# Up projection of a gated MLP in 1024-column groups with one seven-product pair each, its sums on VectorE, and the product of activation and gate on GpSimd

## The chip, the core and the metric

The kernel runs on one core of one Trainium2 chip. A core has five engines with an instruction queue each: TensorE (PE) multiplies 128x128 weights with up to 512 columns into a PSUM bank, VectorE (DVE) and ScalarE (ACT) work element by element on SBUF and PSUM, GpSimd (POOL) on SBUF, and SyncE (SP) here issues most of the DMA transfers. An engine works its queue strictly in order, and an instruction that waits for another engine holds up everything behind it. The metric is the device time of one launch in microseconds.

## What is computed

One layer of a decoder trunk on 256 tokens with a model width of 2048: a mixer of two groups of heads, a gated MLP and a per-layer embedding gate, each added to x. The change is in the MLP, which is, cut from the reference:

```
h = rms_norm(x) @ w_up            # 2048 -> 2 * 5632 columns: a | g
a = causal depthwise convolution of width 3 over the tokens, with bias
u = gelu(a) * g
x = x + u @ w_down                # 5632 -> 2048
```

All is float32.

## The kernel before

**Products.** TensorE takes operands of a rounded type, so each float32 operand is split in two, hi and lo, and a product is three matmuls: hi by hi, hi by lo, lo by hi. The weights stream through SyncE's queue from HBM into a ring of buffers named raw (128 rows of the contraction x 1024 numbers). ScalarE casts a raw to hi (L208), VectorE subtracts to get lo (L210). A block then is 12 matmuls of 512 columns: two halves of the tokens (T1 and T2, 128 each), two halves of the 1024 numbers, three matmuls each. Hi and lo are prepared some blocks ahead of TensorE, `run_stream` decides how many; that distance is called the lead here.

**Up projection.** There are 11 groups q. A group takes 512 columns of a and the same 512 of g, one after the other, with `token_group`: a raw holds two contraction blocks of 128 for 512 columns. So a group is 16 blocks, 8 for a and 8 for g, 192 matmuls; the operand of the tokens is x2T. As either half of a group ends, ScalarE brings its two PSUM banks out with the norm's scale into z (L918), and VectorE transposes them within 32x32 squares into the tile sq (L919).

**The job of a group.** `ffn_job(q)` runs beside the next group's products; two of its pieces are woven in after every block. It sends sq in 16 small transfers Y<-sq on SyncE (L931), so that columns stand on the partitions; ScalarE starts the convolution (L951), VectorE adds the two other taps in eight operations (L954); GpSimd makes the two first positions of each 32 (halo and E, L942 to L948), VectorE adds them (L960); ScalarE applies GELU in place (L962); VectorE multiplies by g in four operations (L966) into u; the split of u into hi (ScalarE, L129) and lo (VectorE, L130) goes into the tile uT. For six pairs of contraction blocks, of the groups 1 to 3 and 6 to 8, sums E3, E5, E6 and E7 of u are made on VectorE (L980) and split into the tile uE (L983, L984).

**Down projection.** After six up groups the first 20 contraction blocks of the down projection are multiplied, after all eleven the other 24, each for 1024 columns twice, with `quad_group`. Here a raw holds one contraction block for 1024 columns. A pair of contraction blocks is either two blocks of 12 (kind R), or a seven-product pair: of the eight products of a 2x2 by 2x2 block multiplication one is saved by sums on both sides (the Winograd form). Such a pair comes in four steps: o1 (two products), o2 (one), c1 (two) and c2 (two). Between o2 and c1 four sums of the raw weights are made in place on VectorE (L357), and c1 and c2 are cast anew from them. The products go to four banks qgD, of the 2x2 halves, and four banks qgQ, which are combined at the end (`down_mid`, L1056 to L1062). `weave` puts the pairs between the R blocks: a head of R blocks, and how many stand between the steps.

**What orders the work.** The instructions of every engine stand in the order in which the code's calls and a scheduler put them; names such as raw_6167 in the rows below number the buffers in order of the code. The rows 380 to 410 and their like are positions in an engine's queue.

Of the kernel before, what the change touches and what calls it, by code (L numbers as in the profile page):

```python
# [15 lines left out]
P = 128  # L16
# [21 lines left out]
QF = 24  # L38
SEVEN = ((3, 5, 7), (13, 15, 17))
PAD = 112  # L40


@with_exitstack
def layer_kernel(
# [18 lines left out]
    def f32(ap):  # L63
        return ap.bitcast(F32)
# [838 lines left out]
    with tc.tile_pool(name="ffn", bufs=1) as fp:  # L903
        uT = fp.tile([P, QF, 512], F32R, name="uT")
        uE = fp.tile([P, max(map(len, SEVEN)), 4, 256], F32R, name="uE")
        in_seven = {p: i for ps_ in SEVEN for i, p in enumerate(ps_)}
        rstd2 = rstd_of(ssq2, "ffn")
        halo = [fp.tile([P, 4, NT, 4, 2], F32, name=f"halo{i}") for i in range(2)]
        for h in halo:
            pool.memset(h, 0.0)  # L910
        sq = {}

        def up_evac(q, ag):
            def f(t, b):
# [3 lines left out]
                act.activation(z, b, AF.Copy, scale=rstd2[:, t : t + 1])  # L918
                dve.transpose(sq[q][:, ag, :, t].rearrange("p j f r -> p f j r"),  # L919
                              z.rearrange("p (f j c) -> p f j c", f=4, j=4))  # L920
                if ag == 1 and t == NT - 1:
                    side.append(ffn_job(q))
            return f

        def ffn_job(q):
# [39 lines left out]
            for f in range(4):  # L965
                dve.tensor_mul(u[:, f], c[:, :, :, f].rearrange("p i t r -> p t i r"),  # L966
                               g[:, :, :, f].rearrange("p i t r -> p t i r"))
            yield
# [3 lines left out]
            for p in (2 * q, 2 * q + 1):  # L972
                if p in in_seven:
# [32 lines left out]
        blocks = []  # L1006
        x2 = aT["cur"]

        def up(q):
            for ag in range(2):  # L1010
                blocks.extend(token_group(w_up, all_k, lambda: x2, ag * FF + q * 512, 512, up_evac(q, ag),
                                          tag=("mm", "aux")[ag]))

        def u_unit(p, name):
            if name[0] == "E":
                v = uE[:, in_seven[p], "3567".index(name[1])]
                return v[:, 0:128], v[:, 128:256]
# [13 lines left out]

        def tmp(i):
            return fp.tile([P, 512], F32, tag="z", name=f"t{i}", bufs=3)

        pT = {}

        def load_p():
            pr = tmp(3).rearrange("p (t d) -> p t d", t=NT)
            nc.sync.dma_start(out=pr, in_=p[0, 0].rearrange("(t p) d -> p t d", p=P))
            yield 6  # L1040
# [4 lines left out]
            pT["t"] = fp.tile([P, 2, 512], F32R, tag="c", name="pT")  # L1045
            for k in range(2):
                split_T(pT["t"][:, k, :], bk[:, k * 256 : (k + 1) * 256])
            yield

        def down_mid(c, ends):  # L1050
            def f(st):
                if ends and c == 0:
                    side.append(load_p())
                xc = [[xs[:, t, (c + n) * 512 : (c + n + 1) * 512] for n in range(2)] for t in range(NT)]
# [24 lines left out]
        def down(pairs, seven, ends, order):  # L1079
            for c in (0, 2):  # L1080
# [3 lines left out]
                cols = w_down[0][:, c * 512 : (c + 2) * 512].rearrange("k (h n) -> k h n", h=2)  # L1084
                tags = ("aux", "mm") if (c == 0) == ends else ("mm", "aux")
                grp = quad_group(lambda k, cols=cols: cols[k * P : (k + 1) * P], seq, u_unit, tags, down_mid(c, ends),
                                 down_end(c, ends))
                if c == 0:
                    st = grp[first]
                    st.fn = lambda hi, lo, fn=st.fn: (pull(10 ** 6), fn(hi, lo))  # L1090
                blocks.extend(grp)
# [13 lines left out]
        def gate_done(c0, n):  # L1105
            sg = {}

            def f(t, b, i=0, j=n):
                if "r" not in r3:
                    r3["r"] = rstd_of(ssq3, "ple")  # L1110
                if i == 0:
                    sg[t] = fp.tile([P, 512], F32, tag="z", name="sg", bufs=3)
                w = (j - i) // (2 if i else 1)
# [46 lines left out]
```

## Time and profile before

| | us |
|---|---|
| median of 3 runs | 1254.61 (1253.37 to 1256.06) |
| the profiled execution | 1254.04 |
| its span, first to last instruction | 1252.2 |
| TensorE busy | 1246.1, 5699 matmuls |
| VectorE busy | 808.4 |
| ScalarE busy | 662.6 |
| GpSimd busy | 35.8 |
| first up group to first down group | 434.2 to 697.2 |
| first down stage | 697.2 to 802.6 |
| up groups 6 to 10 | 802.6 to 1020.2 |
| second down stage | from 1020.2 |

The span is cut by what TensorE multiplies. A busy time is the sum of an engine's instructions; durations of matmuls overlap, so their cost is the distance of their starts. "Idle before" gives what an engine waited for ahead of a group of instructions, and an engine that is waited for by nobody may idle at no cost.

### The profile page before, as it was taken

The numbers are of one execution on the slowest core, as the hardware profiler recorded it, in microseconds if no ns is written. First come the engines' busy times: TensorE is split into PE (matmuls) and PEld (weight loads), VectorE is DVE, ScalarE is ACT, GpSimd is POOL, SyncE is SP. The second block draws the span as 40 slices with busy tenths as digits, with TensorE's granted clock in tenths as the row PEclk, the third lists the DMA queues.
The fourth block names the chain that finished last, engine by engine and source line by source line (L and its number), as shares of the span: only waits on it lengthen the run. The fifth ranks groups of instructions, "written<-read, shape, count | busy, mean of one in ns | idle before, by whom it ended". The sixth has DMA issues, their size and how long they took to land.

```text
span 1252.2 us, 16051 instructions
## 1 busy us (share of the span) xinstructions
PE 1246.1 (100%) x5699; PEld 1048.7 (84%) x5699; DVE 808.4 (65%) x1044; ACT 662.6 (53%) x918; POOL 35.8 (3%) x90
## 2 busy tenths in 40 slices
PE   9999999999999999999999999999999999999998
PEld 7899988888888888888888888888888888888887
DVE  6455566555565555676576697847577659978554
ACT  7555545445554555555465554445455546556542
POOL 2000000000000000000000000000000000000000
PEclk9999999999999999999999999999999999999999
DMA  8667877864567767677777675767767765787661
GB/s 286 173 180 219 255 237 216 209 180 137 162 185 196 236 222 218 202 224 218 212 223 226 186 241 169 234 190 215 231 200 230 222 193 185 222 217 247 205 210 51
DMA packets 161856, 258.77 MB, mean 207 GB/s; under 512 B 38377, under 2 KB 65905, under 8 KB 161777
## 3 DMA queue, kind: packets, MB, share of 16 engines
q1 hardware_dynamic: 161168, 257.57, 68.9%
q8 instruction: 44, 0.72, 0.2%
q14 instruction: 35, 0.29, 0.1%
q10 hardware_dynamic: 385, 0.16, 0.0%
q0 software_dynamic: 224, 0.03, 0.0%
HBM read 237.76 MB, written 2.12 MB: 192 GB/s over the span
## 4 chain that ended last, share of the span: by engine, by line
PE 99%; DMA 0%; SPq 0%; DVE 0%; ACT 0%; issue 0%; DVEq 0%
PE tg L288 26%; PE tg L289 26%; PE tg L290 26%; PE qgD L324 5%; PE qgD L325 5%; PE qgD L326 5%; PE qgQ L325 1%; PE qgQ L324 1%; PE qgQ L326 1%; PE xT L141 1%; PE mob L752 0%; DMA xs<-in_x_dram 0%; PE sc L633 0%; PE ob L661 0%; PE msc L727 0%; PE pt L654 0%
## 5 line engine op out<-in xcount | busy, mean ns | idle before, releaser
L210 DVE TENSOR_TENSOR lo<-raw,hi 128x1024 fp32r<-128x1024 f32 (+3 forms) x475 | 561.4, 1190 | 370.8 <-ACT hi L208 356.4
L208 ACT CAST hi<-raw 128x1024 fp32r<-128x1024 f32 (+3 forms) x475 | 482.6, 1025 | 455.1 <-PE tg L290 304.7
L288 PE MATMUL tg<-hi,x2T 128*128 128x512 f32 x704 | 274.1, 389 | 0.0
L290 PE MATMUL tg<-hi,x2T 128*128 128x512 f32 x704 | 274.0, 389 | 0.0
L289 PE MATMUL tg<-lo,x2T 128*128 128x512 f32 x704 | 273.9, 389 | 0.0
L288 PE MATMUL tg<-hi,hT 128*128 128x512 f32 (+2 forms) x480 | 181.8, 383 | 0.0
L289 PE MATMUL tg<-lo,hT 128*128 128x512 f32 (+2 forms) x480 | 180.3, 378 | 0.0
L290 PE MATMUL tg<-hi,hT 128*128 128x512 f32 (+2 forms) x480 | 180.2, 379 | 0.0
L289 PEld LDWEIGHTS tg<-lo,x2T 128*128 128x128 f32 x704 | 132.1, 188 | 27.5
L290 PEld LDWEIGHTS tg<-hi,x2T 128*128 128x128 f32 x704 | 132.1, 188 | 27.4
L288 PEld LDWEIGHTS tg<-hi,x2T 128*128 128x128 f32 x704 | 132.1, 188 | 27.3
L325 PE MATMUL qgD<-lo,uT 128*128 128x512 f32 x286 | 111.3, 389 | 0.0
L326 PE MATMUL qgD<-hi,uT 128*128 128x512 f32 x286 | 111.2, 389 | 0.0
L324 PE MATMUL qgD<-hi,uT 128*128 128x512 f32 x286 | 103.6, 389 | 0.0
L290 PEld LDWEIGHTS tg<-hi,hT 128*128 128x128 f32 x480 | 89.9, 188 | 12.7
L289 PEld LDWEIGHTS tg<-lo,hT 128*128 128x128 f32 x480 | 90.2, 188 | 12.2
L288 PEld LDWEIGHTS tg<-hi,hT 128*128 128x128 f32 x480 | 90.0, 188 | 12.0
L326 PEld LDWEIGHTS qgD<-hi,uT 128*128 128x128 f32 x286 | 53.7, 188 | 11.2
L324 PEld LDWEIGHTS qgD<-hi,uT 128*128 128x128 f32 x286 | 53.7, 188 | 11.2
L325 PEld LDWEIGHTS qgD<-lo,uT 128*128 128x128 f32 x286 | 53.7, 188 | 11.0
L289 PE MATMUL tg<-lo,x3T 128*128 128x512 f32 (+1 forms) x144 | 52.7, 366 | 0.0
L288 PE MATMUL tg<-hi,x3T 128*128 128x512 f32 (+1 forms) x144 | 52.7, 367 | 0.0
(227 smaller groups left out, 1093.3 us busy)
## 6 DMA issues: line engine op xcount, KB each, us to landing
raw<-in_w_up_dram SPq DMA_DIRECT2D x176, 512.0 KB, 4.6
raw<-in_w_down_dram SPq DMA_DIRECT2D x88, 512.0 KB, 4.7
raw<-in_w_in_dram SPq DMA_DIRECT2D x79, 512.0 KB, 4.3
raw<-in_w_out_dram SPq DMA_DIRECT2D x32, 512.0 KB, 4.3
raw<-in_w_ple_gate_dram SPq DMA_DIRECT2D x32, 512.0 KB, 4.7
Y<-sq SPq DMA_DIRECT2D x176, 64.0 KB, 3.2
raw<-in_w_in_dram SPq DMA_DIRECT2D x24, 416.0 KB, 3.6
raw<-in_w_in_dram SPq DMA_DIRECT2D x16, 408.0 KB, 3.7
```

Source lines behind the costliest of these rows:

```text
L141: pe.transpose(bk[:, t * P : (t + 1) * P], xs[:, t, k * P : (k + 1) * P], ident)
L208: act.copy(hi[:, :w], raw[:, :w])
L210: dve.tensor_sub(lo[:, :w], raw[:, :w], f32(hi[:, :w]))
L288: pe.matmul(bk[:, : e - c], ah, h[:, i, c:e], start=first, stop=False)
L289: pe.matmul(bk[:, : e - c], ah, l[:, i, c:e], start=False, stop=False)
L290: pe.matmul(bk[:, : e - c], al, h[:, i, c:e], start=False, stop=last)
L324: pe.matmul(st[bk], ah, hi[:, cols], start=first, stop=False)
L325: pe.matmul(st[bk], ah, lo[:, cols], start=False, stop=False)
L326: pe.matmul(st[bk], al, hi[:, cols], start=False, stop=final)
```

## The change

The groups q = 1 to 10 of the up projection are made with `quad_group` too: a raw is now one contraction block with 512 columns of a and 512 of g, and the four banks qgD are token half by a or g. Of the eight pairs of contraction blocks, pair 0 is a seven-product pair (`S_UP`), which stands behind four R blocks; its last two steps come after five more R blocks (`UP_ORDER`), and five follow. Its sums of x2 are made once, during group 0 (`x2_sums`, tile x2E). In place of ScalarE's evacuation, `up_mid` combines the four banks qgQ into three tiles and keeps them with the first, all scaled by the norm (ScalarE two operations out of PSUM and three in place, VectorE four out of PSUM), and `up_end` adds each bank qgD, scaled, to one of these (VectorE, four per group), and transposes it. All four banks of a group come to their end in its last block. Group 0 stays as it was.

The product of gelu(a) and g moves from VectorE to GpSimd. The result of the convolution now lies in the g half of the tile sq, which the transfers have emptied, instead of a tile of its own; the temporaries are four of one size; one of the four sums, E3, lies in a place of uT that is not needed (for one pair in uE); p is loaded earlier; the last group of the down projection has a head of five R blocks for four. The line numbers of the changed kernel: hi L211, lo L213, sums of raw L360, `up_mid` L952 to L959, `up_end` L968 and L969, transfers L993, convolution L1013 and L1016, edge L1022, GELU L1024, product L1028, split of u L132 and L133, sums of u L1042 to L1051.

```diff
+ONCE = (7,)
+S_UP = (0,)
+UP_ORDER = (4, (5,))
...
-        uE = fp.tile([P, max(map(len, SEVEN)), 4, 256], F32R, name="uE")
+        uE = fp.tile([P, 10, 256], F32R, name="uE")
...
+        def x2_sums():
+            for i, p in enumerate(S_UP):
+                a = tmp(0).rearrange("p (k s) -> p k s", k=2)
+                e = tmp(1).rearrange("p (e s) -> p e s", e=4)
+                x = x2[:, 2 * p : 2 * p + 2, :]
+                dve.tensor_add(a, f32(x[:, :, 0:256]), f32(x[:, :, 256:512]))
+                a11, a12, a21, a22 = a[:, 0, 0:128], a[:, 1, 0:128], a[:, 0, 128:256], a[:, 1, 128:256]
+                for dst, p0, p1 in ((e[:, 1], a21, a22), (e[:, 3], a21, a11), (e[:, 2], a11, e[:, 1]),
+                                    (e[:, 0], a12, e[:, 2])):
+                    dve.tensor_sub(dst, p0, p1)
+                yield
+                h = x2E[:, i].rearrange("p u (e s) -> p u e s", e=2)
+                act.copy(h[:, :, 0], e)
+                dve.tensor_sub(h[:, :, 1], e, f32(h[:, :, 0]))
+                yield
...
+        def up_mid(q):
+            def f(st):
+                t11, t12, t21, t22 = (tmp(i) for i in range(4))
+                act.copy(t22, st["Q1"])
+                act.activation(t11, st["Q1"], AF.Copy, scale=rstd2[:, 0:1])
+                dve.tensor_sub(t21, st["Q6"], t22)
+                dve.tensor_add(t12, st["Q5"], t21)
+                dve.tensor_add(t21, st["Q7"], t21)
+                dve.tensor_add(t22, st["Q7"], t12)
+                for v, r in ((t12, rstd2[:, 0:1]), (t21, nr[:, 1:2]), (t22, rstd2[:, 1:2])):
+                    act.activation(v, v, AF.Copy, scale=r)
+                comb[q] = (t11, t12), (t21, t22)
+            return f
+
+        def up_end(q):
+            def f(t, ag, b):
+                if t == 0 and ag == 0:
+                    sq[q] = fp.tile([P, 2, 4, NT, 4, 32], F32, tag="sq", name="sq")
+                z = comb[q][t][ag]
+                dve.scalar_tensor_tensor(out=z, in0=b, scalar=rstd2[:, t : t + 1], in1=z, op0=ALU.mult, op1=ALU.add)
+                dve.transpose(sq[q][:, ag, :, t].rearrange("p j f r -> p f j r"),
+                              z.rearrange("p (f j c) -> p f j c", f=4, j=4))
+                if ag == 1 and t == NT - 1:
+                    side.append(ffn_job(q))
+            return f
...
             for f in range(4):
-                dve.tensor_mul(u[:, f], c[:, :, :, f].rearrange("p i t r -> p t i r"),
-                               g[:, :, :, f].rearrange("p i t r -> p t i r"))
+                pool.tensor_tensor(out=u[:, f], in0=c[:, :, :, f].rearrange("p i t r -> p t i r"),
+                                   in1=g[:, :, :, f].rearrange("p i t r -> p t i r"), op=ALU.mult)
...
         def up(q):
-            for ag in range(2):
-                blocks.extend(token_group(w_up, all_k, lambda: x2, ag * FF + q * 512, 512, up_evac(q, ag),
-                                          tag=("mm", "aux")[ag]))
+            if q == 0:
+                for ag in range(2):
+                    blocks.extend(token_group(w_up, all_k, lambda: x2, ag * FF, 512, up_evac(q, ag),
+                                              tag=("aux", "mm")[ag]))
+                return
+            cols = w_up[0].rearrange("k (h n) -> k h n", h=2)[:, :, q * 512 : (q + 1) * 512]
+            seq = weave([p for p in range(KD // 2) if p not in S_UP], S_UP, *UP_ORDER)
+            blocks.extend(quad_group(lambda k: cols[k * P : (k + 1) * P], seq, x2_unit, tags(), up_mid(q), up_end(q)))
...
+        side.append(x2_sums())
         for q in range(6):
             up(q)
         down(range(0, 10), SEVEN[0], False, ((6, (3, 3)), (3, (3, 3, 3))))
         for q in range(6, KF // 4):
             up(q)
-        down(range(10, 22), SEVEN[1], True, ((6, (3, 2, 2)), (4, (3, 3, 3))))
+        down(range(10, 22), SEVEN[1], True, ((6, (3, 2, 2)), (5, (3, 3, 3))))
```

SyncE's queue at a group's end. Before (w_down is the next stage's weight), the transfers of the sixth group:

```order
L239 DMA raw_5989<-in_w_down_dram 128x1024
L931 DMA Y<-sq 32x2x256 x4
L239 DMA raw_6018<-in_w_down_dram 128x1024
L931 DMA Y<-sq 32x2x256 x4
L239 DMA raw_6044<-in_w_down_dram 128x1024
L931 DMA Y<-sq 32x2x256 x8
L239 DMA raw_6158<-in_w_down_dram 128x1024
```

Now, between two up groups:

```order
L242 DMA raw_7652<-in_w_up_dram 128x2x512
L242 DMA raw_7670<-in_w_up_dram 128x2x512
L993 DMA Y<-sq 32x2x256 x16
L242 DMA raw_7849<-in_w_up_dram 128x2x512
L242 DMA raw_7851<-in_w_up_dram 128x2x512
```

The sixteen transfers of an up group now stand in one run, with no weight among them.

VectorE's queue at an up group's end, in the change (t are the combined tiles, qgD the banks):

```order
L968 SCALAR_TENSOR_TENSOR t_5252<-qgD_5012,rstd_ffn,t_5252 128x512
L213 TENSOR_TENSOR lo<-raw_5243,hi 128x1024
L968 SCALAR_TENSOR_TENSOR t_5254<-qgD_5016,rstd_ffn,t_5254 128x512
L969 STREAM_TRANSPOSE sq<-t_5252 128x4x4x32
L968 SCALAR_TENSOR_TENSOR t_5253<-qgD_5020,rstd_ffn,t_5253 128x512
L968 SCALAR_TENSOR_TENSOR t_5255<-qgD_5024,rstd_ffn,t_5255 128x512
L969 STREAM_TRANSPOSE sq<-t_5254 128x4x4x32
L213 TENSOR_TENSOR lo<-raw_5287,hi 128x1024
L969 STREAM_TRANSPOSE sq<-t_5253 128x4x4x32
L969 STREAM_TRANSPOSE sq<-t_5255 128x4x4x32
```

Before, two transposes stood at the end of either half of the group; now four stand at the end of the whole, each behind a scale-and-add.

VectorE's queue in the first down stage, around the second seven-product pair, before:

```order
L966 TENSOR_TENSOR Y<-c,Y 128x256 x4
L210 TENSOR_TENSOR lo<-raw_6176,hi 128x1024
L210 TENSOR_TENSOR lo<-raw_6044,hi 128x512
L130 TENSOR_TENSOR uT<-Y,uT 128x4x256
L357 TENSOR_TENSOR raw_6044<-raw_6044 128x512
L210 TENSOR_TENSOR lo<-raw_6178,hi 128x1024
L357 TENSOR_TENSOR raw_6044<-raw_6044,raw_6158 128x512
L357 TENSOR_TENSOR raw_6158<-raw_6158,raw_6044 128x512
L357 TENSOR_TENSOR raw_6158<-raw_6158 128x512
L210 TENSOR_TENSOR lo<-raw_6044,hi 128x1024
L210 TENSOR_TENSOR lo<-raw_6158,hi 128x1024
```

And now:

```order
L360 TENSOR_TENSOR raw_6167<-raw_6167 128x512
L360 TENSOR_TENSOR raw_6167<-raw_6167,raw_6280 128x512
L133 TENSOR_TENSOR uT<-Y,uT 128x4x256
L360 TENSOR_TENSOR raw_6280<-raw_6280,raw_6167 128x512
L213 TENSOR_TENSOR lo<-raw_6167,hi 128x1024
L360 TENSOR_TENSOR raw_6280<-raw_6280 128x512
L213 TENSOR_TENSOR lo<-raw_6302,hi 128x1024
L213 TENSOR_TENSOR lo<-raw_6322,hi 128x1024
L1131 TENSOR_TENSOR xs<-qgQ_6324,xs 128x512
L213 TENSOR_TENSOR lo<-raw_6280,hi 128x1024
```

The split of u (L130, now L133) stood ahead of the pair's four sums and stands between the second and the third now; c1's lo and c2's (raw_6044 and raw_6158, now raw_6167 and raw_6280) stood together and are apart now, with two lo's and a residual sum between.

More of the change, by code (lines that the diff above doesn't have):

```diff
@@ new lines, in x2_unit @@
+        def x2_unit(p, name):
+            if name[0] == "E":
+                v = x2E[:, S_UP.index(p), "3567".index(name[1])]
+                return v[:, 0:128], v[:, 128:256]
+            t, k = int(name[0]) - 1, 2 * p + int(name[1]) - 1
+            return x2[:, k, t * P : (t + 1) * P], x2[:, k, 256 + t * P : 256 + (t + 1) * P]
+        nr = sm.tile([P, NT], F32, name="nr")
+        dve.tensor_scalar_mul(nr, rstd2, -1.0)
+        comb = {}
+        def up_mid(q):
[11 more added lines that the diff above has]
+            return f
@@ L981, in ffn_job @@
                     yield
-                    w = uE[:, in_seven[p]].rearrange("p u (e s) -> p u e s", e=2)
-                    act.copy(w[:, :, 0], e)
-                    dve.tensor_sub(w[:, :, 1], e, f32(w[:, :, 0]))
+                    n = 3 * in_seven[p]
+                    w = uE[:, n : n + 3].rearrange("p u (e s) -> p u e s", e=2)
+                    v3 = uE[:, 9] if p in ONCE else uT[:, 2 * p % QF]
+                    v3 = v3.rearrange("p (e s) -> p e s", e=2)[:, :, -128:]
+                    act.copy(w[:, :, 0], e[:, 1:4])
+                    act.copy(v3[:, 0], e[:, 0])
+                    dve.tensor_sub(w[:, :, 1], e[:, 1:4], f32(w[:, :, 0]))
+                    dve.tensor_sub(v3[:, 1], e[:, 0], f32(v3[:, 0]))
                     yield
@@ L1039, in load_p @@
             nc.sync.dma_start(out=pr, in_=p[0, 0].rearrange("(t p) d -> p t d", p=P))
-            yield 6
+            while "bank" not in pT:
+                yield 1
             bk = bank("mm", "pTp")
@@ L1052, in f @@
                 if ends and c == 0:
-                    side.append(load_p())
+                    pT["bank"] = True
                 xc = [[xs[:, t, (c + n) * 512 : (c + n + 1) * 512] for n in range(2)] for t in range(NT)]
@@ L1084, in down @@
                 cols = w_down[0][:, c * 512 : (c + 2) * 512].rearrange("k (h n) -> k h n", h=2)
-                tags = ("aux", "mm") if (c == 0) == ends else ("mm", "aux")
-                grp = quad_group(lambda k, cols=cols: cols[k * P : (k + 1) * P], seq, u_unit, tags, down_mid(c, ends),
+                grp = quad_group(lambda k, cols=cols: cols[k * P : (k + 1) * P], seq, u_unit, tags(), down_mid(c, ends),
                                  down_end(c, ends))
@@ L1090, in down @@
                     st.fn = lambda hi, lo, fn=st.fn: (pull(10 ** 6), fn(hi, lo))
+                    if ends:
+                        grp[0].fn = lambda hi, lo, fn=grp[0].fn: (fn(hi, lo), side.append(load_p()))
                 blocks.extend(grp)
+        side.append(x2_sums())
         for q in range(6):
@@ L1111, in f @@
                 if i == 0:
[L1112 removed]
+                    sg[t] = tmp(c0 // 256 + t)
                 w = (j - i) // (2 if i else 1)
```

23 lines of the change are left out of this document (14 added, 9 removed).

## The prediction

> **What bounds the kernel now.** I read the page first: the busy line of the engines and the chain that ended last.
>
> ```profile
> PE 1246.1 (100%) x5699; PEld 1048.7 (84%) x5699; DVE 808.4 (65%) x1044; ACT 662.6 (53%) x918; POOL 35.8 (3%) x90
> PE 99%; DMA 0%; SPq 0%; DVE 0%; ACT 0%; issue 0%; DVEq 0%
> ```
>
> TensorE works in all but 6.1 of the 1252.2 us of the span, and 99% of the chain lies on it. What a matmul costs is read from the timeline, since the mean duration of 389 ns overlaps with its neighbours:
>
> ```profile
> 808.74 0.39 PE L288 MATMUL tg<-hi,x2T 128*128 128x512 f32 x1
> ...
> 810.33 0.39 PE L289 MATMUL tg<-lo,x2T 128*128 128x512 f32 x1
> ```
>
> Seven starts in 1.59 us: one matmul of 512 columns costs 0.2271 us. An up group of 192 takes 192 x 0.2267 = 43.5 us (I use 0.2267, which the distance between the two rows 697.22 and 802.62 of the first down stage, 465 matmuls, gives: 105.4/465). So a matmul that goes away is worth 0.2267 us as long as its successors' operands are ready. Who makes them ready is in the table of stretches and the waits (columns: stretch, PE, PEld, DVE, ACT and POOL busy us with counts, clock, DMA):
>
> ```profile
> 437.00:480.00 43.00, 43.00 (x199) 35.61 (x198) 24.65 (x28) 21.81 (x28) 0.70 (x1) 1.00 0.69 222
> 480.00:523.00 43.00, 43.00 (x192) 35.59 (x191) 27.13 (x35) 24.36 (x27) 1.47 (x5) 1.00 0.73 219
> 523.00:567.00 44.00, 44.00 (x196) 36.44 (x195) 29.29 (x40) 23.55 (x28) 1.37 (x5) 1.00 0.72 215
> 697.00:751.00 54.00, 54.00 (x240) 44.72 (x239) 45.81 (x60) 29.55 (x33) 2.14 (x5) 1.00 0.69 216
> 1020.00:1080.00 60.00, 60.00 (x268) 49.69 (x267) 51.49 (x67) 33.61 (x39) 2.08 (x5) 1.00 0.69 212
> DVE lo L210 <- ACT hi L208: 356.4, 287, 4.6
> ACT hi L208 <- PE tg L290: 304.7, 208, 2.4
> ```
>
> In an up group VectorE works 27 to 29 us of 43.5; in the down stages, which already have seven-product pairs, 45.81 of 54 and 51.49 of 60 (85% and 86%), and TensorE still doesn't stand. The waits run backwards: VectorE waits for ScalarE's hi, and ScalarE for TensorE to free a buffer. The makers are ahead. Clock 1.00 and a DMA share of 0.7 are no bound.
>
> **The change part by part.** *Matmuls.* An up group of 16 blocks of 12 becomes 14 blocks of 12 and a pair of 6 + 3 + 6 + 6 = 21: 189 for 192. Ten groups: 30 matmuls less. 30 x 0.2267 = **-6.8 us**. Nothing else on TensorE changes its number.
>
> *VectorE and ScalarE, per up group.* The rows that price it:
>
> ```profile
> L210 DVE TENSOR_TENSOR lo<-raw,hi 128x1024 fp32r<-128x1024 f32 (+3 forms) x475 | 561.4, 1190 | 370.8 <-ACT hi L208 356.4 <-DMA Y<-sq 7.5 <-DMA raw<-in_w_in_dram 5.2
> L208 ACT CAST hi<-raw 128x1024 fp32r<-128x1024 f32 (+3 forms) x475 | 482.6, 1025 | 455.1 <-PE tg L290 304.7 <-PE qgD L326 52.8 <-DVE raw L357 18.2
> L357 DVE TENSOR_TENSOR raw<-raw,raw 128x512 f32<-128x512 f32 x22 | 15.2, 691 | 0.6
> L966 DVE TENSOR_TENSOR Y<-c,Y 128x256 f32<-128x256 f32 x44 | 15.4, 411 | 0.7 <-ACT c L962 0.7
> L919 DVE STREAM_TRANSPOSE sq<-z 128x512 f32<-128x512 f32 x44 | 31.1, 707 | 6.6 <-ACT z L918 6.6
> L1076 DVE TENSOR_TENSOR xs<-qgD,xs 128x512 f32<-128x512 f32 x8 | 5.3, 681 | 1.1 <-PE qgD L326 1.1
> L1058 DVE TENSOR_TENSOR t<-qgQ,t x4: 682/683/692, 737.1 to 1134.3; 128x512 f32<-128x512 f32 x4
> ```
>
> Lo halves: 17 of 1024 columns and one of 512 for 16, +1.19 + 0.69 = 1.9. Four sums of raw weights at 0.691: 2.8. Four combinations out of PSUM, priced as L1058: 4 x 0.683 = 2.7. Four scale-and-adds out of PSUM, priced as L1076: 2.7. The four products leave: -4 x 0.411 = -1.6. Sum +8.5 us: 36 to 38 of 42.85 us, 84 to 88%. That is the level that the down stages carry now without a stall of TensorE, so throughput costs nothing; the cover is about 5 us per group, and an 11% slower VectorE would use it up. ScalarE has two hi's more, and five operations for the four of L918: 24 to about 26.5 us of 42.85. The sums of x2 (six operations and their halves, once) lie in the first group, where 24.65 of 43 us of VectorE are used: nothing.
>
> *The end of a group.* All four banks of halves finish in the last block now, so four scale-and-adds and four transposes stand together, with two lo's among them: 4 x 0.68 + 4 x 0.70 + 2 x 1.14 = 7.8 us from the first bank, which is done 3/4 of a block, 2.0 us, ahead of the end: the transposes end about 5.8 us into the next group. Only then go the 16 transfers Y<-sq, now in one run on SyncE:
>
> ```profile
> 524.87 2.81 SPq L931 DMA_DIRECT2D Y<-sq  x4
> ...
> 536.33 2.50 SPq L931 DMA_DIRECT2D Y<-sq  x4
> 541.34 2.08 ACT L951 ACTIVATE c<-Y,cT 128x256 f32<-128x256 f32 x4 [3.34 <-DMA Y<-sq]
> ```
>
> Four take 2.50 to 2.81, sixteen 10.0 to 11.2; the convolution starts 2.5 us behind the last issue (541.34 against 536.33 + 2.50). So it starts 18.3 to 19.5 us into the group. Then VectorE's eight (2.88 for seven, row below, so 3.3), the edge 0.2, GELU 1.05, and, where GELU stands ahead of it on ScalarE, the hi of the block behind the pair (1.05) and its lo (1.2): with 0.3 of hand-overs 25.4 to 26.6 us. TensorE reaches that block after 48 + 9 + 60 + 12 = 129 matmuls, 29.2 us. Lead 2.6 us or more: **0** in the up groups, bounds 0 and 2 groups x 1 us.
>
> *The start of a down stage.* Here the product of the last up group is awaited most. The first one before:
>
> ```profile
> 697.22 0.39 PE L324 MATMUL qgD<-hi,uT 128*128 128x512 f32 x1
> 713.11 2.08 ACT L951 ACTIVATE c<-Y,cT 128x256 f32<-128x256 f32 x4 [1.03 <-DMA Y<-sq]
> 719.79 1.05 ACT L962 ACTIVATE c<-c 128x1024 f32<-128x1024 f32 x1
> 721.82 1.42 DVE L966 TENSOR_TENSOR Y<-c,Y 128x256 f32<-128x256 f32 x4
> 724.90 1.22 DVE L130 TENSOR_TENSOR uT<-Y,uT 128x1024 fp32r<-128x1024 f32 x1
> 729.83 4.77 DVE L210 TENSOR_TENSOR lo<-raw,hi 128x1024 fp32r<-128x1024 f32 x4
> 733.94 0.84 PE L324 MATMUL qgQ<-hi,uE 128*128 128x512 f32 x3
> 802.62 0.39 PE L288 MATMUL tg<-hi,x2T 128*128 128x512 f32 x1
> ```
>
> The convolution began 15.9 us into the stage, the split of uT 27.7, and the lo's of the second pair, from 729.83, were done 3 us before their use at 733.94 (36.7 in). Now it begins 2.4 to 3.6 later. The products go to GpSimd, whose price the trace has only for smaller tiles:
>
> ```profile
> L945 POOL TENSOR_TENSOR E<-halo,cT 128x64 f32<-128x64 f32 x11 | 3.6, 325 | 0.9
> L947 POOL TENSOR_TENSOR e<-halo,cT 128x32 f32<-128x32 f32 x11 | 3.0, 272 | 0.0
> ```
>
> 53 ns for 32 elements more: 1.7 ns an element, 0.65 us for 256, four 2.6 us against 1.42. So the split stands at 31.2 to 32.4 and ends at 32.4 to 33.6. Behind it VectorE has, for this pair, one sum and a lo (c1 ready at 34.3 to 35.5, in time for 36.7), then a sum, two lo's, the 0.68 of the residual and c2's lo: 39.2 to 40.4, with its use at 36.7 + 6 x 0.2267 = 38.1. Stall 1.1 to 2.3, **+1.7 us**. In the second down stage the second pair comes earlier, and its lo stands directly behind the split:
>
> ```profile
> 1020.22 0.39 PE L324 MATMUL qgD<-hi,uT 128*128 128x512 f32 x1
> 1054.22 0.61 PE L324 MATMUL qgQ<-hi,uE 128*128 128x512 f32 x2
> ```
>
> Use 34.0 in, ready 33.6 to 34.8: -0.4 to 0.8, and the third pair inherits it: **+0.8**.
>
> *GpSimd beside VectorE.* What the two do to each other shows where GpSimd's copy meets a lo:
>
> ```profile
> 666.53 0.65 POOL L942 COPY halo<-Y 128x48 f32<-128x48 f32 x1 [37.75 <-DMA Y<-sq]
> 665.87 1.23 DVE L210 TENSOR_TENSOR lo<-raw,hi 128x1024 fp32r<-128x1024 f32 x1 [1.50 <-ACT hi L208]
> L942 POOL COPY halo<-Y 128x48 f32<-128x48 f32 x11 | 4.2, 378 | 552.2 <-DMA Y<-sq 552.2
> ```
>
> This copy ends 0.08 us behind the lo, at 0.65 us where the mean is 0.378: GpSimd waits for the lo's end. Below: if every product waits for the rest of one lo, each takes up to 1.2 us, 4.8 for four, +2.2 on the chain. Above: nothing, if they fall in VectorE's gaps. I take nothing here and give the rest to a rival.
>
> The Trainium skill goes further (page "SBUF — State Buffer", section "Who interferes with whom"): a VectorE operation with two inputs in SBUF and a GpSimd operation that reads SBUF shut each other out, and the one that comes later stands until the other is done. The copy's row agrees for GpSimd's side; no row before shows VectorE held for long. By the page VectorE would lose up to the products' 2.6 us per group where 1.6 are saved, and at 1 us more on 38 of 42.85 the sum here would stay as it is; what the lock does to the chain is the second rival.
>
> Loading p earlier, the fourth temporary and the later head of the last group move work off no path that ends last: nothing.
>
> Sum: -6.8 + 1.7 + 0.8 = -4.3. Against the profiled execution's 1254.04 us (its span 1252.2 and 1.8 around it) 1249.7; the median of the runs shown is 0.6 higher, so **1250.3 us**, with 1248 to 1252.5 as this case's own range.
>
> **The rivals.** *No stall at all.* For it: TensorE stood nowhere before at 86% of VectorE, and the down stages' stalls come from sums of 3 us of slip. Against: the lead of 3 us there. Time 1254.6 - 6.8 = 1247.8.
>
> *GpSimd holds VectorE's queue.* In six groups the sums for the down stage read the products, and stand on VectorE about 4.1 us (three lo's and a combination) behind the edge. GELU takes 1.05; products of 1.2 end at 1.4 + 4.8 = 6.2, so VectorE stands 2.1 us with lo's queued behind. Most of it goes into the lead; 0.3 of it on TensorE in six groups is 1.8, and 2.2 later at both down starts is 4.4 at most, half taken: 2.2. -4.3 + 4.0 = -0.3: 1254.3, no change. For it the copy's row; against, that VectorE has gaps of 1.5 us before most lo's (the same rows).
>
> *The transfers come too late, and it is slower.* The 16 transfers stand in one queue behind the last transpose, and weights behind them. If VectorE, at 88%, brings the transposes 5 us later than summed, the block behind the pair is 5 - 2.6 = 2.4 late in the two groups with GELU ahead of its hi, and by about 0.3 in the other eight (their lead is 2.1 us, GELU and a hi, longer: 4.7), 7.2 in all; the two down starts lose 2 to 3 more each, 5. -4.3 + 12.2 = +7.9: **1262.5**. It decides from a slip of 2.6 us. For it: every step of this chain is in order on four queues, and a delay in one group shifts the next. Against: VectorE shows 85% today with no such slip.
>
> **How the numbers follow.** Forecast 42%, no stall 22%, held by GpSimd 20%, late transfers 16%. What the measurement tells from no change is 0.2%, 2.5 us: faster is below 1252.1, slower above 1257.1. Faster: all of no stall, 0.86 of the forecast, a tenth of GpSimd's case, 0.60. Same: the rest of the forecast and three quarters of GpSimd's, 0.21. Slower: late transfers and the rest of GpSimd's, 0.19. The range leaves out the tail below 1246.8 and most of the late transfers: 1246.8 to 1257.5.
>
> **What would show it.** Right: 5669 matmuls on TensorE, the distance of two up groups' first matmuls 42.85 us, VectorE 36 to 38 us in such a stretch, a product on GpSimd of 0.65 us, gaps on TensorE of 1 to 2 us about 38 us into the first down stage and nowhere in the up groups. Wrong: products above 1 us with VectorE waiting for GpSimd by some us in all (GpSimd's case); gaps in every up group 29 us in, with the convolution's wait for Y above 20 us into the group (late transfers); or a VectorE whose lo's last clearly over 1.19 us.

## The result and the profile after

The changed kernel took 1247.01 us (median of 6 runs, 1246.31 to 1248.68) where the kernel before took 1254.26 in the same comparison: a ratio of 0.9943, 95% interval 0.993 to 0.9955, so 0.45 to 0.70% faster. The forecast was 1250.3, with 1248 to 1252.5 as its own range and 1246.8 to 1257.5 in all; the rival without any stall said 1247.8. So the time lies outside the forecast's own range and only 0.2 us inside the wide one. The profiled execution after took 1247.05 us, with a span of 1245.3.

The page of the changed kernel, engines and chain:

```profile
PE 1239.0 (99%) x5669; PEld 1042.4 (84%) x5669; DVE 895.0 (72%) x1153; ACT 682.2 (55%) x955; POOL 92.1 (7%) x134
PE 99%; DMA 0%; SPq 0%; DVE 0%; ACT 0%; issue 0%; DVEq 0%
```

5669 matmuls for 5699, and TensorE still sets the time. The stretches (columns as before), cut at the first matmul of a group or stage:

```profile
564.60:607.60 43.00, 43.00 (x191) 35.44 (x190) 36.20 (x51) 25.62 (x31) 4.89 (x9) 1.00 0.67 208
607.60:650.40 42.80, 42.80 (x190) 35.44 (x189) 37.89 (x52) 25.89 (x31) 6.61 (x9) 1.00 0.71 234
693.20:746.30 53.10, 53.10 (x236) 43.94 (x236) 46.04 (x58) 28.15 (x31) 8.44 (x9) 1.00 0.63 200
1012.80:1076.70 63.90, 63.90 (x284) 52.68 (x284) 58.22 (x72) 35.10 (x41) 7.47 (x9) 1.00 0.65 213
```

The first three rows are the up groups 3 and 4 and the start of the first down stage, the last is the start of the second. An up group takes 42.8 to 43.0 us and TensorE works all of them; VectorE works 36.1 to 37.9 of them in eight of the ten groups (32.4 in group 1, and 29.5 in group 6, beside which no other group's work runs). The whole stretch of the change can be measured between two matmuls: from the first of the up projection to the first of the last projection (operand x3T).

```profile
433.45 0.39 PE L291 MATMUL tg<-hi,x2T 128*128 128x512 f32 x1
1143.25 0.39 PE L291 MATMUL tg<-hi,x3T 128*128 128x512 f32 x1
```

And of the kernel before:

```profile
434.16 0.39 PE L288 MATMUL tg<-hi,x2T 128*128 128x512 f32 x1
1150.18 0.39 PE L288 MATMUL tg<-hi,x3T 128*128 128x512 f32 x1
```

709.80 for 716.02: 6.2 us less. Thirty matmuls are 6.8; 0.6 came back in distances between matmuls of 0.24 to 0.40 us, none longer. The other 0.7 us of the two spans' difference lies ahead of the up projection, whose products the change leaves alone. In the other runs' profiles its first matmul lies anywhere from 433.2 to 435.9, so no gain can be read from these 0.7.

### The profile page after: what moved, and what is told of

Read it like the earlier page. It is cut to its first block, busy times and chain, and to the rows that moved or that the text cites. A ratio compares the mean times of both kernels' runs of the same rounds, so it can differ in the third digit from the quotient of the medians.

```text
span 1245.3 us, 16201 instructions
## 1 busy us (share of the span) xinstructions
PE 1239.0 (99%) x5669; PEld 1042.4 (84%) x5669; DVE 895.0 (72%) x1153; ACT 682.2 (55%) x955; POOL 92.1 (7%) x134
## 4 chain that ended last, share of the span: by engine, by line
PE 99%; DMA 0%; SPq 0%; DVE 0%; ACT 0%; issue 0%; DVEq 0%
PE qgD L327 16%; PE qgD L328 16%; PE qgD L329 16%; PE tg L291 14%; PE tg L293 14%; PE tg L292 14%; PE qgQ L328 2%; PE qgQ L327 2%; PE qgQ L329 2%; PE xT L144 1%; PE mob L755 0%; DMA xs<-in_x_dram 0%; PE sc L636 0%; PE ob L664 0%; PE msc L730 0%; PE pt L657 0%
## 5 line engine op out<-in xcount | busy, mean ns | idle before, releaser
L213 DVE TENSOR_TENSOR lo<-raw,hi 128x1024 fp32r<-128x1024 f32 (+3 forms) x495 | 585.2, 1193 | 284.5 <-ACT hi L211 277.3
L211 ACT CAST hi<-raw 128x1024 fp32r<-128x1024 f32 (+3 forms) x495 | 497.4, 1017 | 434.1 <-PE qgD L329 182.4
L328 PE MATMUL qgD<-lo,x2T 128*128 128x512 f32 x580 | 225.7, 389 | 0.0
L329 PE MATMUL qgD<-hi,x2T 128*128 128x512 f32 x580 | 225.6, 389 | 0.0
L327 PE MATMUL qgD<-hi,x2T 128*128 128x512 f32 x580 | 219.8, 389 | 0.0
L328 PEld LDWEIGHTS qgD<-lo,x2T 128*128 128x128 f32 x580 | 108.9, 188 | 22.7 <-DVE lo L213 0.3
L329 PEld LDWEIGHTS qgD<-hi,x2T 128*128 128x128 f32 x580 | 108.9, 188 | 22.6
L327 PEld LDWEIGHTS qgD<-hi,x2T 128*128 128x128 f32 x580 | 108.9, 188 | 22.6
L329 PE MATMUL qgD<-hi,uT 128*128 128x512 f32 x296 | 115.2, 389 | 0.0
L328 PE MATMUL qgD<-lo,uT 128*128 128x512 f32 x296 | 115.2, 389 | 0.0
L327 PE MATMUL qgD<-hi,uT 128*128 128x512 f32 x296 | 105.9, 390 | 0.0
L327 PEld LDWEIGHTS qgD<-hi,uT 128*128 128x128 f32 x296 | 55.3, 188 | 12.0 <-ACT hi L211 0.7
L329 PEld LDWEIGHTS qgD<-hi,uT 128*128 128x128 f32 x296 | 55.6, 188 | 11.5
L1028 POOL TENSOR_TENSOR Y<-sq,Y 128x256 f32<-128x256 f32 x44 | 50.6, 1180 | 54.5 <-ACT sq L1024 54.5
```

The lines of the kernel that those rows point to most:

```text
L211: act.copy(hi[:, :w], raw[:, :w])
L213: dve.tensor_sub(lo[:, :w], raw[:, :w], f32(hi[:, :w]))
L327: pe.matmul(st[bk], ah, hi[:, cols], start=first, stop=False)
L328: pe.matmul(st[bk], ah, lo[:, cols], start=False, stop=False)
L329: pe.matmul(st[bk], al, hi[:, cols], start=False, stop=final)
L1028: pool.tensor_tensor(out=u[:, f], in0=c[:, :, :, f].rearrange("p i t r -> p t i r"), in1=g[:, :, :, f].rearrange("p i t r -> p t i r"), op ...
```

## Experiments

All times are medians; each ratio is against the kernel before, run beside it on the same chip. A scheduler orders all queues anew for every edit; only in run 6 do TensorE, VectorE and ScalarE work in the same order as in the changed kernel.

**1. The regrouping without the seven-product pair** (the size of a tile, also changed, is left out of the cut).

```diff
-S_UP = (0,)
+S_UP = ()
...
-                z = comb[q][t][ag]
-                dve.scalar_tensor_tensor(out=z, in0=b, scalar=rstd2[:, t : t + 1], in1=z, op0=ALU.mult, op1=ALU.add)
+                z = tmp(2 * ag + t)
+                act.activation(z, b, AF.Copy, scale=rstd2[:, t : t + 1])
```

> The change without its seven-product pair: groups 1 to 10 of the up projection in 1024-column groups of 16 full blocks (192 matmuls again), banks brought out by ScalarE, product on GpSimd. Theory 'the matmuls alone': the changed kernel's 1247.0 plus 30 x 0.2267 = 6.8, so 1253.8, the same as before within 1.5 us. Rival 'the regrouping itself helps' (another lead, other transfers, the relief of VectorE): it stays at 1247 to 1250.

1255.42 us, ratio 1.0013 (1.0004 to 1.0021). The gain is gone with the pair, and 1.6 more than its 6.8 us. TensorE's waits show where: 0.9 and 0.4 us, at the second down stage (two distances of 0.79 and 1.24 us between matmuls, at 1056.2 and 1123.0), which the changed kernel doesn't have there.

```profile
PE qgD L327 <- ACT hi L211: 0.9, 1, 0.9
PE qgQ L328 <- DVE lo L213: 0.4, 1, 0.4
```

**2. The same, with the product back on VectorE**, so that of the change only the regrouping is left, and the small moves of memory and order that go with it:

```diff
-                pool.tensor_tensor(out=u[:, f], in0=c[:, :, :, f].rearrange("p i t r -> p t i r"),
-                                   in1=g[:, :, :, f].rearrange("p i t r -> p t i r"), op=ALU.mult)
+                dve.tensor_mul(u[:, f], c[:, :, :, f].rearrange("p i t r -> p t i r"),
+                               g[:, :, :, f].rearrange("p i t r -> p t i r"))
```

> The regrouped kernel without seven-product pair, with the product back on VectorE: only the regrouping of the up groups is left of the change. Theory 'regrouping costs and brings nothing; the 1.2 us that the regrouped kernel lost lie in its gaps in the second down stage, behind the product on GpSimd': 1254.2 within 1 us, no gap there. Rival 'the regrouping itself costs them': 1255.4.

1255.08 us, 1.0009 (1.0 to 1.0018), one longer distance of 0.93 us at 1119.6. Between the two theories this does not decide: the loss of the first run and of this one cannot be told apart. What both say is that regrouping brings nothing by itself and costs about 1 us (0 to 2.6 by the two intervals).

**3. The changed kernel with its product back on VectorE** (the edit of 2 alone).

> The changed kernel with the four products of each group back on VectorE. Theory 'VectorE's work and the product are covered': 1247.0, within 1.5 us, with VectorE busy 1.6 us more per group from the products and less from lifted contention. Rival 'VectorE needs the relief': 88% becomes 92%, gaps on TensorE in the up groups, 1249 to 1253. Rival 'GpSimd is in the way': faster, 1245, since the chain to the split of u shortens by 3 to 4.5 us at both down starts.

1248.15 us, 0.9953 (0.9939 to 0.9967), against 0.9943 (0.993 to 0.9955): not to be told apart. So the move to GpSimd is not where the gain is from. Against run 2, which differs from this one by the pair alone, the pair is worth 1255.08 - 1248.15 = 6.9 us, where thirty matmuls are 6.8. VectorE's busy time, and one lo here and in the changed kernel:

```profile
PE 1239.1 (99%) x5669; PEld 1042.3 (84%) x5669; DVE 901.0 (72%) x1197; ACT 682.1 (55%) x955; POOL 42.4 (3%) x90
L213 DVE TENSOR_TENSOR lo<-raw,hi 128x1024 fp32r<-128x1024 f32 x432 | 522.6, 1219 | 221.0 <-ACT hi L211 212.2 <-DMA raw<-in_w_in_dram 3.3 <-DMA mkT<-sq 1.9
L213 DVE TENSOR_TENSOR lo<-raw,hi 128x1024 fp32r<-128x1024 f32 x432 | 530.4, 1236 | 233.2 <-ACT hi L211 228.2 <-DMA mqT<-sq 1.5
```

Only 6.0 us more than with the products on GpSimd, though the 44 products keep VectorE busy for 15.7 us in this run. About 10 us of the relief were lost. The rows say where: with the products on GpSimd the lo's take 7.8 us more in all and the sums of raw weights 2.4 more (60.3 for 57.9), both of which read two tiles of SBUF, while the combinations out of PSUM stay at 0.68 us each.

**4. The kernel before with only the product on GpSimd** (the reverse of 2, in the kernel before).

> The kernel before with only the product moved to GpSimd. Theory 'lead decides at the down starts': the chain there grows by 3.3 to 4.5 us against leads of 3.0 and 1.0, so 1 and 3 us are lost: 1254.3 + 4 = 1258. Rival 'the product is off the path wherever it is made': 1254.3 within 1.5 us.

1254.3 us, 0.9995 (0.9986 to 1.0004): no change, and the theory that I favoured, 1258, fell. The chain did get longer (each product 1.04 us for 0.411), but VectorE's and TensorE's queues were ordered anew for it (the third product with uE starts at 735.65, 3.6 us behind the second, where before it stood directly behind it), and the longest distance in the whole MLP is 0.6 us, at its end. A stall that is worked out in the old order isn't the stall of the new one.

```profile
PE 1246.9 (100%) x5699; PEld 1048.4 (84%) x5699; DVE 805.7 (64%) x1000; ACT 662.6 (53%) x918; POOL 81.2 (6%) x134
L966 POOL TENSOR_TENSOR Y<-c,Y 128x256 f32<-128x256 f32 x44 | 44.3, 1040 | 59.5 <-ACT c L962 59.5
```

VectorE lost 15.4 us of products and shows 2.7 less; between runs 2 and 1 it lost 15.7 and shows 3.2 less.

**5. Each product made twice on GpSimd**, first into the free half of sq, then into u.

```diff
+            v = T[:, 0].rearrange("p j t f r -> p (j t f r)").rearrange("p (f t i r) -> p f t i r", f=4, t=NT, i=4)
+            for f in range(4):
+                pool.tensor_tensor(out=v[:, f], in0=c[:, :, :, f].rearrange("p i t r -> p t i r"),
+                                   in1=g[:, :, :, f].rearrange("p i t r -> p t i r"), op=ALU.mult)
             for f in range(4):
                 pool.tensor_tensor(out=u[:, f], ...
```

> The changed kernel with each product made twice on GpSimd (first into the free half of sq, then into u). The chain from GELU to the split of u grows by 2.8 us where VectorE is idle and by up to 5.9 where it is busy. Theory 'small slack at the down starts' (0.4 us and -0.2 us of lead there): 4 us late at each of the two, up groups unharmed, 1247.0 + 8 = 1255, gaps of TensorE about 37 us into the first and 34 us into the second down stage. Rival 'GpSimd's chain is off the path': 1247.0 within 1.5 us. Rival 'contention spreads': VectorE's lo's get longer everywhere and the up groups lose 1 us each, 1257 or more.

1262.13 us, 1.0064 (1.005 to 1.0077): 15 us more than the changed kernel. The theory of the small slack had 8, at the down starts (1255); the rival that contention spreads had 1257 or more. Its stretches there, and in group 3:

```profile
590.00:600.00 10.00, 8.14 (x35) 6.07 (x34) 7.31 (x7) 6.67 (x7) 9.15 (x8) 1.00 0.88 296
720.00:745.00 25.00, 20.86 (x81) 15.79 (x81) 21.14 (x26) 14.71 (x17) 11.11 (x8) 0.93 0.59 199
1057.00:1070.00 13.00, 11.26 (x42) 8.57 (x41) 12.86 (x13) 6.89 (x8) 5.72 (x5) 0.87 0.56 168
```

TensorE stands 1.9 us in up group 3, 4.1 in the first down stage and 1.7 in the second, with another distance of 1.40 at 1127.5. What is new is the clock, 0.93 and 0.87 there: the matmuls behind a stall are slower (below).

**6. The extra work behind the products instead of ahead**, so that nobody waits for it.

```diff
+            v = T[:, 0].rearrange("p j t f r -> p (j t f r)").rearrange("p (f t i r) -> p f t i r", f=4, t=NT, i=4)
+            for f in range(4):
+                pool.tensor_tensor(out=v[:, f], in0=u[:, f],
+                                   in1=g[:, :, :, f].rearrange("p i t r -> p t i r"), op=ALU.mult)
             k = 4 * q % QF
```

> The changed kernel with four more multiplications of the same size per group on GpSimd, u x g into the free half of sq, that nobody reads: they stand behind the products, so the chain to the split of u stays as it is and only GpSimd's work beside VectorE doubles. Theory 'the run with each product made twice lost its 15 us through the longer chain': 1247 to 1250 here, with VectorE's busy time about 12 us up. Rival 'it lost them through VectorE held up by GpSimd': 1255 or more here too.

1256.03 us, 1.0015 (1.0006 to 1.0024): 9 us more than the changed kernel, so neither theory holds alone. No engine waits for the extra products, and the three queues are in the changed kernel's order, so this run shows contention by itself. More than half of the loss in 5 appears here too, though the products' own chain is as long as before; the rest goes with the longer chain. VectorE works 12.0 us more (907.0 for 895.0), as contention was to cost, and the longer distances sit in the same places (at 591, 732, and 1050 to 1055 us, and one of 0.61 at 1124). The first can be followed back. In group 2 the sums of u stand beside the extra products and take up to 0.79 us each for 0.24. VectorE falls behind, so the transfers of group 3 start 2.2 us later than in the changed kernel (there at 570.22), of which 0.5 is the later start of the MLP; the weights behind them come later too, and ScalarE's hi with them:

```profile
L1033 POOL TENSOR_TENSOR sq<-Y 128x256 f32<-128x256 f32 x44 | 57.0, 1324 | 0.0
572.38 10.29 SPq L993 DMA_DIRECT2D Y<-sq  x16
591.36 1.05 ACT L211 CAST hi<-raw 128x1024 fp32r<-128x1024 f32 x1 [1.99 <-DMA raw<-in_w_up_dram]
592.46 1.19 PE L327 MATMUL qgD<-hi,x2T 128*128 128x512 f32 x4 [0.67 <-ACT hi L211]
```

That is the chain of the third rival, late transfers, set off by contention alone.

**7. Two seven-product pairs per up group.** For room in memory the second half of the first down stage gets one pair less, and the sums of x2 and the edge's temporaries get less room (left out of the cut).

```diff
-SEVEN = ((3, 5, 7), (13, 15, 17))
+SEVEN = ((3, 5), (13, 15, 17))
-S_UP = (0,)
-UP_ORDER = (4, (5,))
+S_UP = (0, 1)
+UP_ORDER = (3, (4, 4))
```

> The changed kernel with two seven-product pairs in each of the ten up groups (pairs 0 and 1, three full blocks ahead, four within each pair), and, for room in memory, one pair less in the second half of the first down stage. Matmuls: 30 less in the up groups, 3 more in the down stage, 27 less in all, 6.1 us. VectorE gets two halves and four sums more per group, 1.9 + 2.8 = 4.7 us on 37.6, so 42.3 of 42.2 us. Theory 'covered until VectorE is full': it is full here; the saving is eaten in the groups with sums of u, 1247.0 - 6.1 + 2 to 8 = 1243 to 1249. Rival 'cover is still there' (VectorE's busy time holds waits): 1240.9. Rival 'in-order queues break down': stalls of 2 us or more in every group, above 1255.

1292.15 us, 1.0313 (1.0297 to 1.033): 45 us more than the changed kernel with 27 matmuls less. The rival of queues that break down was right, with stalls of up to 4.7 us. One of them, on ScalarE, VectorE and TensorE:

```profile
640.70 2.07 ACT L1020 ACTIVATE sq<-Y,cT 128x256 f32<-128x256 f32 x4 [4.23 <-DMA Y<-sq]
643.73 3.02 ACT L212 CAST hi<-raw 128x1024 fp32r<-128x1024 f32 x3
641.34 2.11 DVE L1023 SCALAR_TENSOR_TENSOR sq<-Y,cT,sq 128x248 f32<-128x248 f32 x5 [3.42 <-ACT sq L1020]
643.37 0.69 DVE L361 TENSOR_TENSOR raw<-raw,raw 128x512 f32<-128x512 f32 x1
644.82 2.26 PE L328 MATMUL qgD<-hi,x2T 128*128 128x512 f32 x4 [4.70 <-ACT hi L212]
```

ScalarE stood 4.23 us for the transfers with three hi's queued behind; VectorE stood 3.42 us for ScalarE with a sum of raw weights behind; TensorE then had no hi.

**8. Thirty-two transfers for sixteen**, each of half the size, in the changed kernel.

```diff
-                    nc.sync.dma_start(out=Y[32 * j : 32 * j + 32, :, i], in_=T[32 * i : 32 * i + 32, :, j])
+                    for h in range(2):
+                        nc.sync.dma_start(out=Y[32 * j : 32 * j + 32, h, i], in_=T[32 * i : 32 * i + 32, h, j])
```

> The changed kernel with each of the 16 transfers Y<-sq cut into two of half the size, so 32 in one run of about 20 us on SyncE where 16 took 10.3. The convolution starts 10 us later in every group and the weights behind the run are issued 10 us later. Theory 'the transfers have little slack' (lead of the block behind the pair 3.4 us in most groups, 0 in groups 3 and 8): 5 to 7 us lost in each of ten groups, 1247.0 + 60 = 1300 and more. Rival 'the chain of transfers has slack': the weights were loaded ahead and only the down starts lose, 10 us each less 0.4: 1266.

1317.83 us, 1.0508 (1.0493 to 1.0522): 71 us more. So the third rival's mechanism is real, and its slack is small: a run of 20.23 us for 10.3 stalls nearly every up group. On SyncE's queue and ScalarE:

```profile
575.37 20.23 SPq L994 DMA_DIRECT2D Y<-sq  x32
595.70 12.20 SPq L242 DMA_DIRECT2D raw<-in_w_up_dram  x9
596.91 2.08 ACT L1014 ACTIVATE sq<-Y,cT 128x256 f32<-128x256 f32 x4 [6.63 <-DMA Y<-sq]
600.00 1.05 ACT L211 CAST hi<-raw 128x1024 fp32r<-128x1024 f32 x1 [1.01 <-DMA raw<-in_w_up_dram]
```

The convolution and the weights were late both; the time is set by the issue, since the bytes are the same and one of the run's transfers takes 0.63 us of it for 0.64.

**9. Every second transfer issued by ScalarE**, in the changed kernel.

```diff
-                    nc.sync.dma_start(out=Y[32 * j : 32 * j + 32, :, i], in_=T[32 * i : 32 * i + 32, :, j])
+                    (nc.sync, nc.scalar)[j % 2].dma_start(out=Y[32 * j : 32 * j + 32, :, i], in_=T[32 * i : 32 * i + 32, :, j])
```

> The changed kernel with every second of the 16 transfers Y<-sq issued by ScalarE, so the run on SyncE is 8 long, about 5 us for 10.3. Theory 'the chain of transfers has slack of some us in the changed kernel': no gap is there to be taken away, 1247.0 within 1.5 us; the convolution's wait for Y gets shorter, and the lead of the block behind the pair grows in groups 3 and 8 if the weights behind the run limited it, and stays near 0 if the ring of six raws did. Rival 'ScalarE's issue costs its queue': 8 x 0.6 us more on ScalarE, hi's late, 1249 or more.

1258.79 us, 1.0031 (1.0022 to 1.004): slower by 11.8 than the changed kernel; the rival was right.

```profile
527.98 6.89 ACTq L993 DMA_DIRECT2D Y<-sq  x8
534.97 4.85 ACT L211 CAST hi<-raw 128x1024 fp32r<-128x1024 f32 x5 [6.37 <-PE qgD L329]
```

For 6.9 us ScalarE issues and casts nothing; five hi's then come at once. The up groups bear it, the down starts don't (distances of up to 1.72 us at 717 to 723 and 1.71 at 1041 to 1047, and one of 1.90 at 1123.6).

**10. All transfers issued by GpSimd.**

```diff
-                    nc.sync.dma_start(out=Y[32 * j : 32 * j + 32, :, i], in_=T[32 * i : 32 * i + 32, :, j])
+                    nc.gpsimd.dma_start(out=Y[32 * j : 32 * j + 32, :, i], in_=T[32 * i : 32 * i + 32, :, j])
```

> The changed kernel with all 16 transfers Y<-sq issued by GpSimd, so no weight stands behind them on SyncE. Theory as for the two queues: 1247.0 within 1.5 us if GpSimd issues as fast as SyncE. Rival 'GpSimd issues more slowly, or is held while VectorE works': the convolution starts later, and the gaps of the run with 32 transfers come back, 1260 or more.

1261.63 us, 1.0057 (1.0042 to 1.0072). The time is the rival's, but not its reason: an issue on GpSimd takes 0.54 us, less than SyncE's 0.59, and the long distances lie at the second down stage, hardly in the up groups. The longest, 3.77 us at 1063.7, follows a chain that is late from its start: VectorE's last transpose ends 14.0 us into that stage, for 5.6 in the changed kernel, because in the new order the split of the group before and three lo's stand among the scale-and-adds and transposes, and VectorE waits 3.1 us for that split; then the four products take 7.19 us for 5.07. What the issue by GpSimd does change is the landing: a transfer lands 4.7 us behind its issue in the median, where SyncE's land after 2.0. How much of the loss that is, and how much the new order, stays open.

**11. Two pairs, with every second transfer issued by ScalarE** (the edits of 7 and 9).

> The kernel with two pairs in each up group (27 matmuls less than the changed kernel), with every second of the transfers Y<-sq issued by ScalarE. The first run of two pairs took 1292, with ScalarE waiting 35.3 us for Y with hi's queued behind. Theory 'the late transfers made most of its loss': the convolution starts 5 us sooner, most gaps close, 1245 to 1260. Rival 'VectorE is full' (41 to 42 us of 42.2 in a group): it stays above 1275.

1294.31 us, 1.031 (1.0293 to 1.0327), as slow as 7. The cure shortens the wait that it was meant for and brings no time: the convolutions wait 3.0 us for Y where they waited 35.3, but ScalarE is now idle for 62.4 us ahead of ten hi's, in which it issues transfers. One of the ten:

```profile
626.63 6.73 ACTq L1000 DMA_DIRECT2D Y<-sq  x8
633.46 1.04 ACT L212 CAST hi<-raw 128x1024 fp32r<-128x1024 f32 x1 [7.92 <-DMA Y<-sq]
```

So the late transfers are neither shown nor refuted as the cause of 7's loss: this cure costs ScalarE what it gives. Whether VectorE, with the 42 of 42.2 us that were summed for it, would break it alone stays open, since every run with two pairs also has late transfers.

## Why the prediction was right, and what was wrong in it

The forecast was right in its main term and wrong in both of its stalls, 1.7 and 0.8 us, which did not come; without them its sum is the measured time within 0.8 us. That nothing stalled was in part luck, as the up groups and the down starts show.

- **The matmuls**, -6.8: right. Thirty went, 0.2267 us each; the up groups measure 42.8 to 43.0 for 42.85 forecast. Run 1 shows that without the pair nothing of the gain is left, and runs 2 and 3 give the pair 6.9.
- **VectorE covered at 84 to 88%**: right. 36.1 to 37.9 us where 36 to 38 were summed, and no longer distance of matmuls. By these numbers VectorE could be 13% slower, 42.85 for 38, not 11%. How near the limit is, run 7 does not tell, since its transfers were late as well.
- **The up groups' chain**: the cost of 0 came true, its reason did not. The convolution was to start 18.3 to 19.5 us into the group; in group 3 it starts at 582.76, 18.2 in. But the lead of 2.6 us was not there. "48 + 9 + 60 + 12 = 129 matmuls, 29.2 us" counts five full blocks ahead of the pair's last two steps. Four stand there, one behind o1 and three behind o2; the fifth of `UP_ORDER` is the block behind the pair itself, and five more follow it. So TensorE reaches that block after 117 matmuls, 26.5 us in. And the chain left out that ScalarE waits for a weight that stands behind the sixteen transfers:

```profile
589.65 1.05 ACT L211 CAST hi<-raw 128x1024 fp32r<-128x1024 f32 x1 [1.72 <-DMA raw<-in_w_up_dram]
590.74 2.50 DVE L213 TENSOR_TENSOR lo<-raw,hi 128x1024 fp32r<-128x1024 f32 x2 [3.96 <-ACT hi L211]
591.11 1.07 PE L327 MATMUL qgD<-hi,x2T 128*128 128x512 f32 x4
592.02 0.50 PE L328 MATMUL qgD<-lo,x2T 128*128 128x512 f32 x1
```

  The hi was ready 0.41 us ahead of its first matmul, and the first lo, at 591.96, 0.06 us: next to no lead. Four products of hi had been drawn ahead of the first lo, which gave the lo 0.7 us. That nothing was lost here was luck; 1.7 us on this chain in run 6 were enough for a stall.
- **The first down start**, +1.7: wrong, it cost nothing. The chain was summed well: the convolution starts 19.3 in (18.3 to 19.5 summed), the split of u stands at 33.2 in (31.2 to 32.4), c2's lo is done 40.7 in (39.2 to 40.4). The step that failed is "its use at 36.7 + 6 x 0.2267 = 38.1". I took TensorE's order from the order of the code. TensorE's own queue has c2's products elsewhere:

```profile
693.24 0.39 PE L327 MATMUL qgD<-hi,uT 128*128 128x512 f32 x1
...
729.96 0.62 PE L327 MATMUL qgQ<-hi,uE 128*128 128x512 f32 x2
...
734.04 0.39 PE L327 MATMUL qgQ<-hi,uE 128*128 128x512 f32 x1
736.53 0.39 PE L328 MATMUL qgQ<-lo,uE 128*128 128x512 f32 x1
```

```profile
726.41 1.23 DVE L133 TENSOR_TENSOR uT<-Y,uT 128x1024 fp32r<-128x1024 f32 x1 [1.71 <-ACT uT L132]
732.76 1.22 DVE L213 TENSOR_TENSOR lo<-raw,hi 128x1024 fp32r<-128x1024 f32 x1
```

  c1 is used at 729.96, 36.7 in, as worked out. But twelve matmuls of other blocks stand between c1 and c2, and within c2 the hi product is drawn ahead of others still: the lo, ready at 733.98, is first read at 736.53, 43.3 in. The scheduler that had moved the lo back on VectorE had moved its reader back on TensorE as well.
- **The second down start**, +0.8: wrong for the same reason in small. c1's first matmul is at 1046.84, 34.0 in, as forecast, but seven hi products stand ahead of the first lo product at 1048.55, 35.7 in. The lo was due at 33.6 to 34.8 and was done 34.5 in.

```profile
1046.84 0.84 PE L327 MATMUL qgQ<-hi,uE 128*128 128x512 f32 x3
1047.52 1.19 PE L327 MATMUL qgD<-hi,uT 128*128 128x512 f32 x4
1048.55 0.40 PE L328 MATMUL qgQ<-lo,uE 128*128 128x512 f32 x1
```

- **The product on GpSimd**, 0.65 us each: right only beside an idle VectorE. The two ends, in group 3 and in the first down stage, and the mean:

```profile
588.01 2.82 POOL L1028 TENSOR_TENSOR Y<-sq,Y 128x256 f32<-128x256 f32 x4 [4.01 <-ACT sq L1024]
719.37 5.92 POOL L1028 TENSOR_TENSOR Y<-sq,Y 128x256 f32<-128x256 f32 x4 [4.58 <-ACT sq L1024]
L1028 POOL TENSOR_TENSOR Y<-sq,Y 128x256 f32<-128x256 f32 x44 | 50.6, 1180 | 54.5 <-ACT sq L1024 54.5
```

  0.70 us where VectorE stands, 1.48 where it works, 1.18 in the mean: the rival's price of up to 1.2 was the better one. It cost no time because the readers were placed late, not because the price was small: doubling it cost 15 us (run 5), 9 of them by contention alone (run 6).
- **GpSimd beside VectorE, taken as nothing**: as a time right, as a size wrong. The page "SBUF — State Buffer", section "Who interferes with whom", of the Trainium skill says that either may be held; here VectorE was held as well, about 10 us over the kernel in run 3 and 13 in run 4, and a sum of raw weights that takes 0.69 us took 1.22 while a product ran:

```profile
705.70 0.69 DVE L360 TENSOR_TENSOR raw<-raw 128x512 f32<-128x512 f32 x1
722.33 1.22 DVE L360 TENSOR_TENSOR raw<-raw 128x512 f32<-128x512 f32 x1
```

- **The rival that came true** is the one without a stall, 1247.8, which I gave 22%. The two others name mechanisms that runs 5, 6 and 8 show to be real, with little slack: they did not decide here. Of the signs of being right, the matmuls, the distance of the groups and VectorE's share came, the price of 0.65 us and the gaps at the down start did not; of the GpSimd rival's signs, products above 1 us came, without its loss of time.

## What to carry to other kernels

When a scheduler orders the queues, a stall must be worked out with the reader's place taken from the reader's own queue in the changed order, matmul by matmul, and not from the order of the code; at the down starts here, and in run 4, a maker that moved back took its reader along. Count the blocks ahead of a reader there as well: one block too many hid that a chain had no lead. A saving of TensorE's work is kept as long as every maker has lead, but the lead is bought from queues that are in order: here one more pair per group, ten more microseconds of small transfers, or a second round of work on GpSimd turned a gain of 7 us into a loss of 2 to 64. Work that is moved from VectorE to GpSimd relieved VectorE here by far less than its own duration, 2.7 to 6.0 us of about 15.5.

## What the runs showed of the chip that I had not expected

A stall of TensorE costs more than its length. In run 8 TensorE stood from 548.5 on, and its clock then showed, by stretch:

```profile
540.00:548.00 8.00, 8.00 (x37) 6.64 (x36) 0.90 (x1) 0.82 (x2) 0.91 (x4) 1.00 0.20 51
552.00:556.00 4.00, 3.13 (x8) 1.92 (x8) 4.00 (x9) 3.70 (x6) 0.00 (x0) 0.50 1.03 386
560.00:562.00 2.00, 2.00 (x10) 1.68 (x9) 2.00 (x2) 0.00 (x0) 2.00 (x2) 1.00 0.95 333
```

After a distance of 3.16 us the granted clock was 0.50, matmuls came every 0.427 us for 0.227, and only some 7 us later was it full again. Over the run, in the stages of the MLP, 76 matmuls came so slowly, 15 us on top of 48 us of stalls. The length of a single distance does not decide: one of 2.08 us (run 5, at 590.6) had no such effect, while one of 1.71 with two shorter ones behind it (run 6, at 1050.1) did. The clock records of the traces show what does. Within a run every stretch at half clock begins and ends on a grid of 3.413 us, and lasts one step of it or two (3.41 or 6.83 us). Runs 5 to 11 have 24 such stretches in the MLP. Counting each matmul as 0.227 us, TensorE was filled to at most 37% in the grid step ahead of each of the 24, and none of the 1512 other steps that began at full clock was filled to less than 39%. The 2.08 us fell across two steps, of which the first was filled to 55%; most of the 1.71 us and their two followers lay in one step, filled to 34%. The page "TensorE: Matmul & The Clock Gate" of the Trainium skill, Part 1, has the halved clock after an idle window of about 3.4 us, which runs freely. The step of 3.413 us and its grid agree with it; the idle window does not, since here steps that were filled to as much as 37% were enough.
